# Seven block products for eight in the projections of a two-layer decoder trunk, with the first mixer in two stages and the last projection in one

## The chip, the cores and the metric

The kernel runs on one core of a Trainium2 chip. The metric is device time in microseconds (us) of one execution; three runs stand for the kernel before. The engines are TensorE (PE: matmuls, and transposes as matmuls), VectorE (DVE), ScalarE (ACT), GpSimd (POOL) and SyncE (SP, which issues the loads and stores). [...]

## The reference

1024 tokens of 1024 channels, with 16 learned meta tokens ahead of them (1040 in all), pass two layers, each with a norm ahead and a residual add behind. All is float32.

```python
hn = rmsnorm(h, norm_w[0])                     # layer 0: pooling mixer
v, gate = jnp.split(hn @ w_in, 2, axis=-1)     # w_in 1024 x 4096
u = trailing_mean(v, window 2/4/8/16 by group) - v
u = jnp.einsum('blgc,gcd->blgd', u, w_grp) * scale      # 4 groups of 512
h = h + (u * silu(gate)) @ w_out               # w_out 2048 x 1024
hn = rmsnorm(h, norm_w[1])                     # layer 1: HGRN2, 16 heads of 128
q, f, i, gate = jnp.split(hn @ w_in, 4, axis=-1)        # w_in 1024 x 8192
f = lb + (1 - lb) * sigmoid(f);  k = (1 - lb) * sigmoid(-f)
S_t = diag(f_t) S_{t-1} + k_t i_t^T;  o_t = S_t^T silu(q_t)
o = rmsnorm per head(o) * o_norm
h = h + (o * silu(gate)) @ w_out               # w_out 2048 x 1024
out = rmsnorm(h[16:], final_norm_w)
```

## The kernel before

Each float32 operand is split into hi + lo, both exact in the matmul's type: ACT casts hi (L209), DVE subtracts for lo (L210). A product is then three matmuls, whi with xhi, whi with xlo, wlo with xhi (`mm3`, L204 to L206). Tokens stand in the free dimension, channels in the partitions. x, transposed and split, lies in `xhi` and `xlo` for all of layer 0, the normed hn in the same place for layer 1; weights are prepared two ahead (`tick`, `need`).

Layer 0 (`mixer0`) goes by groups: four v tiles of 128 columns of w_in with their pooling (`v_tile`), then twice two gate tiles, their group projection (`grp_part`) and their part of the out projection, added into `acc` in SBUF (`out_part`, L360). Each tile takes the tokens in three chunks of 400, 384 and 256 columns (`CH0`), 24 matmuls each (8 channel blocks x 3), and a bank of PSUM for each chunk; four banks (`mm`) are for this, four (`at`) for transposes and the recurrence. `between` transposes h, makes the second norm, keeps h in DRAM and splits hn.

Layer 1 (`mixer1`) has 16 heads with four tiles each, f and i over all tokens in `CH0`, q and g in two chunks of 512. The recurrence of a head is cut into pieces (running product of the gates L601 and its reciprocal L602, scores L617, rectangles L573, turned K, states L700, outputs L719 and L720, gated output L734 to L737), which `later` places in the slots between the next head's projections. The gated output goes to `a_dram`. The last projection runs over heads 0 to 7 for all tokens and then over heads 8 to 15, with the weights of one half in SBUF (L781 to L783); behind each token tile of the second half come the final norm and the store.

The order on each engine is that of the program as the framework's scheduler leaves it; engines wait for one another by semaphores.

Of the kernel before, what the change touches and what calls it, by code (L numbers as in the profile page):

```python
# [8 lines left out]
F32 = mybir.dt.float32  # L9
# [5 lines left out]
P = 128  # L15
D = 1024
# [5 lines left out]
E = 2048  # L22
WINDOWS = (2, 4, 8, 16)
# [5 lines left out]
HALO = 16  # L29
# slots behind a head's last projection at which the pieces of its recurrence are issued  # L30
SCAN = (0, 1, 2, 3, 5, 7)
# [7 lines left out]
def kernel(  # L39
# [17 lines left out]
    vec, act, pool, pe = nc.vector, nc.scalar, nc.gpsimd, nc.tensor  # L57

    cst = ctx.enter_context(tc.tile_pool(name="cst", bufs=1))
    big = ctx.enter_context(tc.tile_pool(name="big", bufs=1))  # L60
    wp = ctx.enter_context(tc.tile_pool(name="wp", bufs=3))
    ps_mm = ctx.enter_context(tc.tile_pool(name="ps_mm", bufs=4, space=bass.MemoryType.PSUM))
    ps_at = ctx.enter_context(tc.tile_pool(name="ps_at", bufs=4, space=bass.MemoryType.PSUM))

# [3 lines left out]
    def mmbank():  # L68
        return ps_mm.tile([P, 512], F32, tag="mm", name="mm")
# [14 lines left out]
    def rstd_into(r, ssq, tn, n, dim):  # L84
        vec.tensor_scalar(r[:tn, :n], ssq[:tn, :n], 1.0 / dim, EPS, ALU.mult, ALU.add)  # L85
        pool.tensor_tensor(r[:tn, :n], r[:tn, :n], nhalf[:tn, :n], ALU.pow)  # L86
# [5 lines left out]
    stage = cst.tile([P, 4, HALO + L], F32, tag="stage", name="stage")  # L92
    raws = cst.tile([P, 2, 1024], F32, tag="raws", name="raws")
    nraw = [0]

    def ring(pool_, n, first=0):
        # n buffers in turn, the first four on the staging tile
        slots = [stage[:, i] for i in range(4)]
        slots += [pool_.tile([P, HALO + L], F32, tag=f"t{i}", name="t") for i in range(4, n)]
        at = [first]  # L100

        def get(name):
            at[0] += 1
            return slots[(at[0] - 1) % n]

        return get

    # per-channel vectors, turned so that the channel is the partition
    def load_tok(i, xt):
        t0, tn = TT[i]  # L110
        nc.sync.dma_start(xt[:tn], meta_tokens if i == 0 else x[t0 - META : t0 - META + tn])
        return xt

    w_in0 = pool_w_in[0].rearrange("(k p) n -> p k n", p=P)
    vr = [raws[:48, 1, :P], raws[:32, 1, P : 2 * P]]
    toks = {}
    nc.sync.dma_start(vr[0][0:32], hgrn_lb_logits.rearrange("a (k p) -> (a k) p", p=P))
    nc.sync.dma_start(vr[0][32:48], norm_w.rearrange("a (k p) -> (a k) p", p=P))
    toks[0] = load_tok(0, stage[:, 0, :D])
    toks[1] = load_tok(1, stage[:, 1, :D])  # L120
    nc.sync.dma_start(raws[:, 0].rearrange("p (a b) -> p a b", b=P), w_in0[:, :, :P])
    toks[2] = load_tok(2, stage[:, 2, :D])
    toks[3] = load_tok(3, stage[:, 3, :D])
# [74 lines left out]
    def prep_w(views, scale=None):  # L198
        return split_w(load_w(views), scale)
# [666 lines left out]
```

## Time and profile before

| | |
|---|---|
| runs | 1802.2, 1802.86 (median), 1804.11 us |
| span of the profiled execution | 1802.3 us |
| PE busy | 1778.4 us, 99% of the span |
| DVE, ACT, POOL busy | 1032.2 (57%), 551.5 (31%), 47.9 us (3%) |
| matmuls of the projections (L204 to L206) | 25% of the chain for each of the three lines |
| moved through HBM | 88.71 MB read, 16.78 MB written, 59 GB/s |
| granted clock of PE, mean | 0.998 |

Busy time of PE is modelled from pipelined matmuls, and a matmul's listed duration overlaps the next one's. What a matmul costs in a row of them is the distance between two starts. [...]

### The profile page before, as it was taken

What the parts mean: (1) busy time and instruction counts of PE and PEld (TensorE: products, weight loads), DVE (VectorE), ACT (ScalarE), POOL (GpSimd) and SP (SyncE); (2) the same over time, 40 slices, a digit from 0 to 9 for tenths busy, and PEclk for the clock granted to TensorE, in tenths of its full rate; (3) what the DMA queues carried; (4) which work ended last, traced back from release to release, by engine and by line L of the source; (5) the groups of instructions that cost most, each with busy time, mean ns of one, the idle gap of its engine ahead of it and who ended that gap; (6) DMA issues with size and microseconds to landing.
All of it is one profiled execution on the core that took longest, in us unless ns stands there. A gap on an engine that the chain in (4) does not pass through costs nothing.

```text
span 1802.3 us, 26333 instructions
## 1 busy us (share of the span) xinstructions
PE 1778.4 (99%) x11015; PEld 1649.4 (92%) x11015; DVE 1032.2 (57%) x1720; ACT 551.5 (31%) x1372; POOL 47.9 (3%) x68
## 2 busy tenths in 40 slices
PE   7999999999999999999999999999999999999998
PEld 7999999999999988899988999898989999888886
DVE  6765665685577568645564465546564555553433
ACT  6222322221222245232323333243323332232221
POOL 1000000000000000000000000000000000000000
PEclk9999999999999999999999999999999999999999
DMA  4111111111111113111111111121111111143421
GB/s 155 57 33 53 48 48 48 47 47 36 47 52 55 48 71 114 40 47 52 53 38 47 48 47 36 48 83 47 48 47 47 47 48 36 47 140 97 126 94 61
DMA packets 133823, 107.26 MB, mean 60 GB/s; under 512 B 3424, under 2 KB 122288, under 8 KB 133696
## 3 DMA queue, kind: packets, MB, share of 16 engines
q1 hardware_dynamic: 133696, 105.50, 19.0%
q8 instruction: 88, 1.44, 0.3%
q14 instruction: 39, 0.32, 0.1%
HBM read 88.71 MB, written 16.78 MB: 59 GB/s over the span
## 4 chain that ended last, share of the span: by engine, by line
PE 96%; ACT 1%; DVE 1%; POOL 0%; issue 0%; DMA 0%; SPq 0%; POOLq 0%; DVEq 0%; ACTq 0%
PE mm L204 25%; PE mm L206 25%; PE mm L205 25%; PE mm L781 3%; PE mm L783 3%; PE mm L782 3%; PE at L573 2%; PE at L700 2%; PE at L720 2%; PE at L617 2%; PE at L719 2%; PE at L539 1%; PE at L734 1%; PE at L684 1%; POOL rstd L86 0%
## 5 line engine op out<-in xcount | busy, mean ns | idle before, releaser
L204 PE MATMUL mm<-xhi,whi 128*128 128x400 f32 (+3 forms) x2048 | 704.0, 344 | 0.7 <-ACT xhi L209 0.7
L205 PE MATMUL mm<-xlo,whi 128*128 128x400 f32 (+3 forms) x2048 | 696.3, 340 | 0.2
L206 PE MATMUL mm<-xhi,wlo 128*128 128x400 f32 (+3 forms) x2048 | 695.9, 340 | 0.0
L204 PEld LDWEIGHTS mm<-xhi,whi 128*128 128x128 f32 x2048 | 385.3, 188 | 25.3 <-ACT xhi L209 1.3
L206 PEld LDWEIGHTS mm<-xhi,wlo 128*128 128x128 f32 x2048 | 386.2, 189 | 22.5
L205 PEld LDWEIGHTS mm<-xlo,whi 128*128 128x128 f32 x2048 | 385.7, 188 | 22.7 <-DVE xlo L210 0.9
L210 DVE TENSOR_TENSOR wlo<-raws,whi 128x1024 fp32r<-128x1024 f32 x88 | 107.5, 1222 | 116.8 <-ACT whi L209 116.7
L209 ACT CAST whi<-raws 128x1024 fp32r<-128x1024 f32 x88 | 92.4, 1050 | 257.6 <-PE mm L205 257.6
L360 DVE TENSOR_TENSOR acc<-acc,mm 128x400 f32<-128x400 f32 (+2 forms) x192 | 97.4, 514 | 57.9 <-PE mm L206 57.1
L204 PE MATMUL mm<-ah,whi 128*128 128x400 f32 (+2 forms) x384 | 124.8, 325 | 0.0
L205 PE MATMUL mm<-al,whi 128*128 128x400 f32 (+2 forms) x384 | 123.5, 322 | 0.0
L206 PE MATMUL mm<-ah,wlo 128*128 128x400 f32 (+2 forms) x384 | 123.1, 321 | 0.0
L192 ACT ACTIVATE whi<-raws,vecs 128x128 fp32r<-128x128 f32 x256 | 78.3, 390 | 143.2 <-PE mm L205 133.8
L86 POOL TENSOR_TENSOR rstd<-rstd,nhalf 128x1 f32<-128x1 f32 (+2 forms) x42 | 43.0, 1024 | 1705.0 <-DVE rstd L85 1702.4
L193 DVE SCALAR_TENSOR_TENSOR wlo<-raws,vecs,whi 128x128 fp32r<-128x128 f32 x256 | 75.2, 345 | 4.6 <-ACT xhi L166 2.8
L204 PEld LDWEIGHTS mm<-ah,whi 128*128 128x128 f32 x384 | 72.6, 189 | 0.2 <-DVE acc L360 0.2
L206 PEld LDWEIGHTS mm<-ah,wlo 128*128 128x128 f32 x384 | 72.7, 189 | 0.0
L205 PEld LDWEIGHTS mm<-al,whi 128*128 128x128 f32 x384 | 72.7, 189 | 0.0
L785 DVE TENSOR_TENSOR hres<-hres,mm 128x512 f32<-128x512 f32 x32 | 21.9, 686 | 85.6 <-PE mm L783 85.6
L736 DVE SCALAR_TENSOR_TENSOR G<-at,vecs,G 128x512 f32<-128x512 f32 x32 | 22.6, 746 | 82.9 <-PE at L734 82.9
L504 DVE TENSOR_SCALAR F<-F,oml,lb 128x400 f32<-128x400 f32 (+2 forms) x48 | 21.6, 454 | 73.0 <-ACT F L502 73.0
L206 PE MATMUL mm<-uh,wlo 128*128 128x400 f32 (+2 forms) x192 | 61.7, 321 | 0.0
(192 smaller groups left out, 2391.8 us busy)
## 6 DMA issues: line engine op xcount, KB each, us to landing
raws<-in_hgrn_w_in_dram SPq DMA_DIRECT2D x64, 512.0 KB, 3.9
raws<-in_pool_w_in_dram SPq DMA_DIRECT2D x32, 512.0 KB, 3.9
raws<-in_pool_w_out_dram SPq DMA_DIRECT2D x16, 512.0 KB, 3.6
a_dram<-G SPq DMA_DIRECT2D x16, 512.0 KB, 2.9
araw<-a_dram SPq DMA_DIRECT2D x16, 512.0 KB, 4.2
raws<-in_hgrn_w_out_dram SPq DMA_DIRECT2D x16, 512.0 KB, 3.9
raws<-in_pool_w_grp_dram SPq DMA_DIRECT2D x8, 512.0 KB, 3.3
hres<-h_dram SPq DMA_DIRECT2D x8, 512.0 KB, 4.2
```

The lines of the kernel that those rows point to most:

```text
L86: pool.tensor_tensor(r[:tn, :n], r[:tn, :n], nhalf[:tn, :n], ALU.pow)
L192: act.activation(hi[:, s], raw[:, s], AF.Copy, scale=scale[:, k : k + 1])
L193: vec.scalar_tensor_tensor(lo[:, s], raw[:, s], scale[:, k : k + 1], hi[:, s].bitcast(F32), ALU.mult, ALU.subtract)
L204: pe.matmul(ps, lhsT=wh, rhs=xh, start=i == 0, stop=False)
L205: pe.matmul(ps, lhsT=wh, rhs=xl, start=False, stop=False)
L206: pe.matmul(ps, lhsT=wl, rhs=xh, start=False, stop=i == n - 1)
L209: act.copy(hi, src)
L210: vec.tensor_tensor(lo, src, hi.bitcast(F32), ALU.subtract)
L360: vec.tensor_tensor(acc[:, m, s], acc[:, m, s], ps[:, :cn], ALU.add)
L781: pe.matmul(ps, lhsT=ah[:, n], rhs=wh[:, ws], start=n == 0, stop=False)
L782: pe.matmul(ps, lhsT=ah[:, n], rhs=wl[:, ws], start=False, stop=False)
L783: pe.matmul(ps, lhsT=al[:, n], rhs=wh[:, ws], start=False, stop=n == 7)
```

## The change

The input projections of both layers become block products. Two column tiles of weights (v and gate of one index, q and g, or f and i of one head) and the eight channel blocks make a matrix of 2 x 2 blocks (A); the channels in two halves and the tokens of one half of all (520) in two chunks of 260 columns (`CH`) make another (B). `pair` makes the seven weight operands, four of them with additions of 512 columns on DVE, `make_T` the seven token operands in hi + lo, which stay in SBUF for all tiles. `products` runs the seven in the order of `PRODUCTS`, both token halves with the same weights: 4 channel blocks x 3 matmuls x 2 chunks. Two double banks of PSUM take them: P1, P6, P7 and P4 add up in one, P2, P5 and P3 in the other, and after each product ACT copies or DVE adds what stands there.

```diff
-CH0 = ((0, 400), (400, 384), (784, 256))
-CHQ = ((16, 512), (528, 512))
+CH = 260
+PT = 2 * CH
...
+PRODUCTS = ("P1", "P2", "P6", "P5", "P7", "P3", "P4")
+OPENS = ("P1", "P2", "P5")
+BANK_A = ("P1", "P6", "P7", "P4")
...
+LOOK = 3
...
+        def pair(view1, view2):
+            i1, i2 = rawid(view1), rawid(view2)
+            st = {}
...
+            def p1():
+                ensure(i2)
+                return split_w(blocks()[0])
+            def p2():
+                return split_w(blocks()[1])
+            def p6():
+                a11, a12, a21, a22 = blocks()
+                s1, s2 = (half(n).rearrange("p a b -> p (a b)")[:, :512] for n in ("S1", "S2"))
+                st["s1"], st["s2"] = s1, s2
+                vec.tensor_tensor(s1, a21, a22, add)
+                vec.tensor_tensor(s2, s1, a11, sub)
+                return split_w(s2)
...
+            def p5():
+                ensure(i2 + 1)
+                return split_w(st["s1"])
+            def p7():
+                a11, a12, a21, a22 = blocks()
+                vec.tensor_tensor(a21, a11, a21, sub)
+                return split_w(a21)
...
+            def p3():
+                a11, a12, a21, a22 = blocks()
+                vec.tensor_tensor(a12, a12, st["s2"], sub)
+                return split_w(a12)
...
+        def make_T(p, src, R, w):
...
+            def norm(i):
+                t = unit("hn").rearrange("p (k t) -> p k t", k=2)
+                for j in range(2):
+                    k = 2 * i + j
+                    vec.scalar_tensor_tensor(t[:, j], src[i][:, j], w[:, k : k + 1], R, mul, mul)
+                hn[i] = t.rearrange("p k (c t) -> p k c t", c=2)
...
+            def put(name, srcs):
+                hi, lo = (unit(f"T{s}", F32R).rearrange("p (k t) -> p k t", k=4) for s in "hl")
+                for i, s in enumerate(srcs):
+                    n = s.shape[1]
+                    split(hi[:, i * n : (i + 1) * n], lo[:, i * n : (i + 1) * n], s)
+                T[name][p] = (hi, lo)
...
+            def s1():
+                norm(0), norm(1)
+                put("P1", B(0, 0))
+
+            def s2():
+                norm(2), norm(3)
+                put("P2", B(1, 0))
+
+            def s3():
+                diff("1", B(0, 1), B(0, 0))
+                diff("2", B(1, 1), halves(d["1"]))
+                put("P6", [d["2"]])
+
+            def s4():
+                put("P5", [d["1"]])
+                diff("4", B(1, 0), halves(d["2"]))
+
+            def s5():
+                diff("3", B(1, 1), B(0, 1))
+                put("P7", [d["3"]])
+
+            def s6():
+                put("P3", B(1, 1))
+                put("P4", [d["4"]])
+
+            return [s1, s2, s3, s4, s5, s6]
+        def products(passes, m, m2):
+            s = slice(passes[0], passes[-1] + 1)
+            a = x_ = None
+            for name in PRODUCTS:
+                w = need()
+                if name == "P1":
+                    a = mmbanks()
+                elif name == "P2":
+                    x_ = mmbanks()
+                b = a if name in BANK_A else x_
+                for p in passes:
+                    th, tl = T[name][p]
+                    for k in range(4):
+                        ks = slice(k * P, (k + 1) * P)
+                        o = b[:, p, :CH]
+                        first = name in OPENS and k == 0
+
+                        kw = dict(skip_group_check=True)
+                        pe.matmul(o, lhsT=w[:, 0, ks], rhs=th[:, k], start=first, stop=False, **kw)
+                        pe.matmul(o, lhsT=w[:, 0, ks], rhs=tl[:, k], start=False, stop=False, **kw)
+                        pe.matmul(o, lhsT=w[:, 1, ks], rhs=th[:, k], start=False, stop=k == 3, **kw)
+                bs = b[:, s, :CH]
+                if name in ("P1", "P6", "P5"):
+                    t = half(name)
+                    act.copy(t[:, s], bs)
+                    if name == "P1":
+                        p1 = t
+                    elif name == "P6":
+                        u2 = t
+                    else:
+                        p5 = t
+                elif name == "P2":
+                    m(s, 0, bs, p1[:, s])
+                elif name == "P7":
+                    m2(s, 1, bs, p5[:, s])
+                elif name == "P3":
+                    m(s, 1, bs, u2[:, s])
+                else:
+                    m2(s, 0, bs, None)
+                tick()
```

Norm weights go into the token operands, not into the weights. Layer 0 first makes v and gate of all 16 pairs, and keeps the pooled u and the gate in DRAM (`u_dram`, `s_dram`). Then, for one token half after the other, `grp_stage` makes the group projection and `out_stage` the out projection, both with chunks of 260; their weights are loaded for each half. x comes back from `x_dram`. The second norm of the first half is spread over the second half's stages, that of the second half over head 0.

```diff
+        def grp_stage(p):
+                for k in range(4):
+                    ur = half("ur").rearrange("p a b -> p (a b)")
+                    nc.sync.dma_start(ur, u_dram[g * 4 + k][:, p * PT : (p + 1) * PT])
+                    u = unit("u", F32R).rearrange("p (h t) -> p h t", h=2)
+                    split(u[:, 0], u[:, 1], ur)
+                    us.append(u)
+                for j in range(4):
+                    w = need()
+                    sg = half("sgh")
+                    m = g * 4 + j
+                    nc.sync.dma_start(sg.rearrange("p a b -> p (a b)"), s_dram[m][:, p * PT : (p + 1) * PT])
+                    ps = mmbanks()
+                    mm3(ps, w, us, True, True)
+                    vec.scalar_tensor_tensor(sg, ps[:, :, :CH], pscale[:, m : m + 1], sg, mul, mul)
+                    at = unit("a", F32R).rearrange("p (h t) -> p h t", h=2)
+                    split(at[:, 0], at[:, 1], sg.rearrange("p a b -> p (a b)"))
+                    a[m] = at
+                    tick()
...
+        def out_stage(p, a):
+            for m in range(KD):
+                    h = unit("h").rearrange("p (k t) -> p k t", k=2)
+                    nc.sync.dma_start(h, x_dram[m : m + 2, :, p * PT : (p + 1) * PT].rearrange("k p t -> p k t"))
+                ps = mmbanks()
+                for q in range(4):
+                    mm3(ps, need(), [a[4 * q + i] for i in range(4)], q == 0, q == 3)
+                    tick()
+                o = hs[-1][:, m % 2].rearrange("p (c t) -> p c t", c=2)
+                vec.tensor_tensor(o, o, ps[:, :, :CH], add)
...
+        steps = prologue(1)
+        spread(steps)
+        c0 = v_gate(0)
+        products((0,), *c0)
+        flush()
+        products((1,), *c0)
+        for t in range(1, ME):
+            products((0, 1), *v_gate(t))
+        flush()
+        a = grp_stage(0)
+        hs = out_stage(0, a)
+        spread(between(0, hs))
+        a = grp_stage(1)
+        hs = out_stage(1, a)
+        flush()
+        mixer1(between(1, hs))
```

In layer 1 the gate g of a head goes to `g_dram`, and the output `og` without it to `a_dram`. The last projection takes all 16 heads in one accumulation, in four blocks of 256 tokens, and loads and multiplies a and g for each head and block; the weights are loaded and split in the first block. The reciprocals are four of 260 columns (L693).

```diff
-                    vec.scalar_tensor_tensor(G[:, s], b, onorm[:, n : n + 1], G[:, s], mul, mul)
-                nc.sync.dma_start(a_dram[n], G)
+                        act.activation(og[:, b0 * P : b0 * P + 512], b, AF.Copy, scale=onorm[:, n : n + 1])
+                    nc.sync.dma_start(a_dram[n], og)
...
+                    for i in range(4):
+                        s = slice(i * CH, (i + 1) * CH)
+                        vec.reciprocal(iX[:, s], X[:, s])
...
+            def prep(r, n):
+                if r == 0:
+                    raw = rawtile()
+                    nc.sync.dma_start(raw, hgrn_w_out[0, n * P : (n + 1) * P])
+                    wh, wl = unit("woh", F32R), unit("wol", F32R)
+                    split(wh[:, :D], wl[:, :D], raw)
+                    wo[n] = (wh, wl)
+                ar, gr = (half(t).rearrange("p a b -> p (a b)")[:, :256] for t in ("ar", "gr"))
+                ts = slice(r * 256, r * 256 + 256)
+                nc.sync.dma_start(ar, a_dram[n][:, ts])
+                nc.sync.dma_start(gr, g_dram[n][:, META + r * 256 : META + r * 256 + 256])
+                vec.tensor_tensor(ar, ar, gr, mul)
+                w = wslot()
+                split(w[:, 0, :256], w[:, 1, :256], ar)
+                return w
...
+            for r in range(NR):
+                ps = None
+                for n in range(HEADS):
+                    fetch(r * HEADS + n + 3)
+                    if ps is None:
+                        if r % 2 == 0:
+                            ps = [[t[:, 0], t[:, 1]] for t in (mmbanks(), mmbanks())]
...
+                    for i in range(2):
+                        ts = slice(i * P, (i + 1) * P)
+                        for nh in range(2):
+                            s = slice(nh * 512, nh * 512 + 512)
+                            pe.matmul(ps[i][nh], lhsT=w[:, 0, ts], rhs=wh[:, s], start=n == 0, stop=False)
+                            pe.matmul(ps[i][nh], lhsT=w[:, 0, ts], rhs=wl[:, s], start=False, stop=False)
+                            pe.matmul(ps[i][nh], lhsT=w[:, 1, ts], rhs=wh[:, s], start=False, stop=n == HEADS - 1)
```

How rows move on the engines, at three places:

PE, the first instructions behind the branch. L164 and L400 are transposes of x, L214 and L151 the broadcast of a token's norm, L204 to L206 the first tile. Before:

```order
L164 MATMUL at<-ident,stage 128x16 x8
L164 MATMUL at<-ident,stage 128x128 x8
L134 MATMUL at<-ident,raws 128x32
L164 MATMUL at<-ident,stage 128x128 x16
L204 MATMUL mm<-xhi,whi 128x400
L205 MATMUL mm<-xlo,whi 128x400
L214 MATMUL at<-ident,rstd 128x16
L206 MATMUL mm<-xhi,wlo 128x400
L204 MATMUL mm<-xhi,whi 128x400
L205 MATMUL mm<-xlo,whi 128x400
L206 MATMUL mm<-xhi,wlo 128x400
L204 MATMUL mm<-xhi,whi 128x400
```

Now (L338 to L340 are the first product, of the first token half):

```order
L400 MATMUL at<-ident,xt 128x16 x8
L151 MATMUL at<-ident,rstd 128x16
L400 MATMUL at<-ident,xt 128x128 x8
L151 MATMUL at<-ident,rstd 128x128
L400 MATMUL at<-ident,xt 128x128 x8
L151 MATMUL at<-ident,rstd 128x128
L400 MATMUL at<-ident,xt 128x128 x8
L151 MATMUL at<-ident,rstd 128x128
L400 MATMUL at<-ident,xt 128x120 x8
L151 MATMUL at<-ident,rstd 128x120
L338 MATMUL mm<-Th,w 128x260
L339 MATMUL mm<-Tl,w 128x260
```

Before, the first tile's matmuls stand between the broadcasts; now all transposes and broadcasts of a half stand ahead of its first product, whose right operand (`Th`, `Tl`) is made from the normed tokens.

DVE, the hand-over from one group to the next in the group projection. L344 and L486 scale the product and multiply with the gate, L210 and L147 are the subtractions for lo. Before, at the first chunks of a group:

```order
L344 SCALAR_TENSOR_TENSOR stage<-mm,vecs,stage 128x400
L210 TENSOR_TENSOR al<-stage,ah 128x400
L287 MEMSET stage 128x16
L344 SCALAR_TENSOR_TENSOR stage<-mm,vecs,stage 128x400
L210 TENSOR_TENSOR al<-stage,ah 128x400
L344 SCALAR_TENSOR_TENSOR stage<-mm,vecs,stage 128x384
L210 TENSOR_TENSOR al<-stage,ah 128x384
L344 SCALAR_TENSOR_TENSOR stage<-mm,vecs,stage 128x384
```

Now, at the end of one group (`a`, `w`: gated product and weights; `u`: the operands of the next group):

```order
L486 SCALAR_TENSOR_TENSOR sgh<-mm,vecs,sgh 128x520
L147 TENSOR_TENSOR w<-raw,w 128x512
L147 TENSOR_TENSOR a<-sgh,a 128x520
L486 SCALAR_TENSOR_TENSOR sgh<-mm,vecs,sgh 128x520
L147 TENSOR_TENSOR w<-raw,w 128x512
L147 TENSOR_TENSOR a<-sgh,a 128x520
L147 TENSOR_TENSOR u<-ur,u 128x520 x4
L486 SCALAR_TENSOR_TENSOR sgh<-mm,vecs,sgh 128x520
L147 TENSOR_TENSOR w<-raw,w 128x512
L147 TENSOR_TENSOR a<-sgh,a 128x520
```

The four u subtractions of the next group stand behind the last gated product of this one; before, u of a group was split a tile at a time behind its pooling.

DVE, a head's scan and reciprocals (L601 and L602 before, L690 and L693 now), with F's last gate ahead and q behind. Before:

```order
L504 TENSOR_SCALAR F<-F,oml,lb 128x256
L599 COPY Zt<-F 128x65
L600 MEMSET F 128x65
L601 SCALAR_TENSOR_TENSOR stage<-F,Zt 128x1040
L602 RECIPROCAL stage<-stage 128x1040
L517 SCALAR_TENSOR_TENSOR Q<-mm,oml,stage 128x512
L704 COPY stage<-at 128x128
L606 TENSOR_TENSOR K<-K,stage 128x1040
```

Now (`P_` numbers are copied products, `mm` the bank; L633 and L636 make F, L611 and L613 q of the next head):

```order
L147 TENSOR_TENSOR w<-S_8878,w 128x512
L633 TENSOR_TENSOR F<-P_8696,mm 128x2x260
L147 TENSOR_TENSOR w<-raw,w 128x512
L636 TENSOR_SCALAR F<-F,oml,lb 128x2x260
L688 COPY Zt<-F 128x65
L689 MEMSET F 128x65
L690 SCALAR_TENSOR_TENSOR X<-F,Zt 128x1040
L147 TENSOR_TENSOR w<-raw,w 128x512
L693 RECIPROCAL F<-X 128x260 x4
L611 TENSOR_TENSOR Q<-P_8913,mm 128x2x260
L696 TENSOR_TENSOR Q<-Q,X 128x1024
L613 SCALAR_TENSOR_TENSOR Q<-Q,oml,sig 128x2x260
```

Behind the reciprocals now stands the add of the next head's first q product from its bank, and a weight subtraction stands between scan and reciprocals.

## Rows read from the trace of the kernel before

**Rows 1.** The page's list of busy engines, and its group of POOL's powers:

```profile
PE 1778.4 (99%) x11015; PEld 1649.4 (92%) x11015; DVE 1032.2 (57%) x1720; ACT 551.5 (31%) x1372; POOL 47.9 (3%) x68
...
L86 POOL TENSOR_TENSOR rstd<-rstd,nhalf 128x1 f32<-128x1 f32 (+2 forms) x42 | 43.0, 1024 | 1705.0 <-DVE rstd L85 1702.4
```

**Rows 2.** Windows: busy us (and count) of each engine, clock, DMA:

```profile
0.00:36.00 36.00, 26.59 (x140) 22.74 (x141) 20.17 (x59) 26.18 (x62) 8.07 (x31) 1.00 0.48 164
640.00:700.00 60.00, 54.35 (x337) 49.33 (x336) 42.39 (x96) 34.10 (x82) 5.56 (x9) 0.97 0.28 97
726.90:785.10 58.20, 58.20 (x379) 52.62 (x379) 31.60 (x42) 18.33 (x50) 1.65 (x1) 1.00 0.16 46
```

**Rows 3.** Timeline of PE in layer 0: start, duration, line, shape:

```profile
100.46 0.34 PE L204 MATMUL mm<-uh,whi 128*128 128x384 f32 x1
...
104.67 0.34 PE L204 MATMUL mm<-ah,whi 128*128 128x400 f32 x1
...
113.31 0.28 PE L204 MATMUL mm<-uh,whi 128*128 128x256 f32 x1
...
115.67 0.28 PE L206 MATMUL mm<-uh,wlo 128*128 128x256 f32 x1
```

**Rows 4.** Timeline of PE, one column tile of head 1:

```profile
729.72 0.39 PE L205 MATMUL mm<-xlo,whi 128*128 128x512 f32 x1
...
735.05 0.34 PE L204 MATMUL mm<-xhi,whi 128*128 128x400 f32 x1
```

**Rows 5.** The chain of waits, start and length of its pieces:

```profile
677.24 1.71 PE at L395 x8
...
726.88 1.78 PE at L617 x16
...
785.09 1.78 PE at L617 x16
```

**Rows 6.** Timeline of PE in the last projection, to its last matmul:

```profile
1785.21 0.39 PE L781 MATMUL mm<-wo_h,ah 128*128 128x512 f32 x1
...
1786.34 0.39 PE L783 MATMUL mm<-wo_h,al 128*128 128x512 f32 x1
...
1793.14 0.39 PE L783 MATMUL mm<-wo_h,al 128*128 128x512 f32 x1
```

**Rows 7.** Timeline of DVE in one head:

```profile
741.93 0.69 DVE L564 TENSOR_TENSOR Q<-Q,Fe 128x512 f32<-128x512 f32 x1 [1.29 <-PE at L573]
742.54 0.68 DVE L565 TENSOR_TENSOR K<-K,Fe 128x512 f32<-128x512 f32 x1
...
752.64 2.33 DVE L601 TENSOR_TENSOR_SCAN stage<-F,Zt 128x1040 f32<-128x1040 f32 x1
755.00 6.65 DVE L602 RECIPROCAL stage<-stage 128x1040 f32<-128x1040 f32 x1
```

**Rows 8.** DVE by line and shape: busy us, mean ns, idle before:

```profile
L210 DVE TENSOR_TENSOR wlo<-raws,whi 128x1024 fp32r<-128x1024 f32 x88 | 107.5, 1222 | 116.8 <-ACT whi L209 116.7
```

**Rows 9.** DMA issues: queue, count, size, us to landing:

```profile
raws<-in_hgrn_w_in_dram SPq DMA_DIRECT2D x64, 512.0 KB, 3.9
...
a_dram<-G SPq DMA_DIRECT2D x16, 512.0 KB, 2.9
...
t<-in_x_dram SPq DMA_DIRECT2D x2, 512.0 KB, 5.5
```

**Rows 10.** ACT by line and shape, the gates' sigmoid:

```profile
L516 ACT ACTIVATE stage<-mm 128x512 f32<-128x512 f32 x18 | 10.7, 597 | 31.8 <-PE mm L206 31.8
```

**Rows 11.** Windows, the stretch that moves most bytes:

```profile
6.00:10.00 4.00, 2.84 (x16) 2.40 (x16) 1.81 (x5) 2.29 (x8) 0.00 (x0) 1.00 1.07 410
```

**Rows 12.** Timeline of PE at the start:

```profile
17.14 0.54 PE L204 MATMUL mm<-xhi,whi 128*128 128x400 f32 x1
...
18.80 0.54 PE L206 MATMUL mm<-xhi,wlo 128*128 128x400 f32 x1
```

More of the change, by code (lines that the diff above doesn't have):

```diff
@@ L22 @@
 E = 2048
+ME = E // P
 WINDOWS = (2, 4, 8, 16)
@@ L382, in between, with load_tokens @@
-        def between(c0, cn):
-            tiles = [(t0, tn) for t0, tn in TT if c0 <= t0 < c0 + cn]
-            rb = None
-            for t0, tn in tiles:
-                ssq, r = small("ssq"), small("rstd", 6)
-                if not hts:
-                    hts.extend(t0tile("ht") for _ in range(4))
-                hts.append(hts.pop(0))
-                ht = hts[0]
+        def load_tokens(p):
+            out_ = []
+            for t0, tn in TP[p]:
+                xt = unit("xt")
+                if t0 == 0:
+                    nc.sync.dma_start(xt[:tn, :D], meta_tokens)
+                else:
+                    nc.sync.dma_start(xt[:tn, :D], x[t0 - META : t0 - META + tn])
+                out_.append(xt)
+            return out_
@@ new lines, in mm3 @@
+        def mm3(ps, w, xs, first, last):
+            for k in range(4):
+                ks = slice(k * P, (k + 1) * P)
+                for c in range(2):
+                    cs = slice(c * CH, (c + 1) * CH)
+                    o = ps[:, c, :CH]
+                    pe.matmul(o, lhsT=w[:, 0, ks], rhs=xs[k][:, 0, cs], start=first and k == 0, stop=False)
+                    pe.matmul(o, lhsT=w[:, 0, ks], rhs=xs[k][:, 1, cs], start=False, stop=False)
+                    pe.matmul(o, lhsT=w[:, 1, ks], rhs=xs[k][:, 0, cs], start=False, stop=last and k == 3)
@@ new lines, in spread, with flush, early @@
+        def spread(steps, gap=1, first=0):
+            for i, fn in enumerate(steps):
+                later(first + i * gap, fn)
+        def flush():
+            while due:
+                now[0] += 1
+                for fn in due.pop(now[0] - 1, []):
+                    fn()
+        def early(n, tiles, view):
+            for t in list(range(n)) * 2 + list(range(n, tiles)):
+                pair(*view(t))
+        early(1, ME, lambda t: (cols(w_in0, t), cols(w_in0, ME + t)))
+        for _ in range(2):
+            feed_grp()
+            feed_out()
@@ new lines, in whole @@
+        early(1, 2 * HEADS, lambda t: head_views(t // 2)[t % 2])
+        for fn in prologue(0):
+            fn()
+        fill()
+        if fast:
+            later(40, make_mask)
+        steps = prologue(1)
+        spread(steps)
+        c0 = v_gate(0)
[4 more added lines that the diff above has]
+            products((0, 1), *v_gate(t))
+        flush()
+        a = grp_stage(0)
+        hs = out_stage(0, a)
+        spread(between(0, hs))
```

1096 lines of the change are left out of this document (495 added, 601 removed).

## The prediction

> **What bounds the kernel now.** I read the page's busy list first: TensorE (PE) has 1778.4 of 1802.3 us, VectorE (DVE) 57% [rows 1]. The table by windows says where the missing 24 us lie: PE is full in a stretch such as one head (58.20 of 58.20), and is not in the first 36 us (26.6) and from 640 to 700 us (54.4) [rows 2]; the rest lies behind the last matmul. So the kernel lasts as long as its matmuls, and a matmul as long as its step, start to start. That I read from the timeline: 24 steps of 384 columns take 4.21 us (0.175), 48 of 400 take 8.64 (0.180), 20 of 256 take 2.36 (0.118) [rows 3]; in a head 23 steps of 512 take 5.33 (0.232) [rows 4]. Weight loads are inside these steps. The chain of waits meets the same line of successive heads 58.2 us apart [rows 5].
>
> Before, in these terms: layer 0 has 32 tiles x 24 x (0.180 + 0.175 + 0.118) = 363.6 us, its group projection 192 x 0.473 = 90.9, its out projection 384 x 0.473 = 181.8; together 636.3. A head is 24 x (2 x 0.473 + 4 x 0.232) = 45.0 of projections; the remaining 13.2 of 58.2 are pieces of the recurrence. The last projection is 768 steps of 0.226 = 173.6 (5 take 1.13), and from the end of the last matmul, 1793.5, to the end 8.8 pass [rows 6]. Going back from the end (8.8, 173.6, 1 between, 16 x 58.2) head 0 begins near 687.5. So layer 0 has 687.5 - 636.3 = 51 us that are not its projections: start, transposes, second norm.
>
> **The change, part by part.**
>
> *Products.* A pair of column tiles needs 7 products of 24 matmuls of 260 columns. The trace has no 260; between 256 and 400 a column costs 0.43 ns, so 0.118 + 0.0017 = 0.1197 us. Bounds: 0.118, no dearer than 256, and 0.122, since the step of 384 lies 2.3 ns over that line. A pair takes 168 x 0.1197 = 20.1 us. Layer 0: 16 pairs, 321.8 for 363.6, **-41.8**. Heads: 32 pairs, 643.5 for 16 x 45.0 = 719.5, **-76.0**. Group and out projection in the same chunks: 2304 x 0.1197 = 275.8 for 272.7, **+3.1**. The bounds shift all of this by -18 to +24. The last projection keeps 768 matmuls of 512 columns. The arithmetic alone gives -115.
>
> *The start.* Work moves to DVE. Per half of the tokens the operands take 8 norms, 8 differences and 6 subtractions of 520 columns and 4 subtractions of 1040. Back to back 512 columns take 0.61 [rows 7]; 1024 have a duration of 1.22 [rows 8], so a step near 1.15: 22 x 0.62 + 4 x 1.15 = 18 us. The tokens are loaded only behind the branch (near 6 us), land 5.5 us later [rows 9], and pass transposes, a square sum, POOL's power and a broadcast: the first norm starts near 22 us. From there DVE has 2 x 18 us of operands, 2.5 weight sets of 11 instructions at 0.61 (17 us), and copies, small ones and adds (8): 61 us. The first product of tile 1 needs the second half's operands, so it starts near 83. Of that time 20 us are tile 0's products: 63 of overhead. Bounds 45, if the second half's operands are done in step with the products, and 75. Tiles of window 16, the ones with most adds, cost some 2 more.
>
> *Two stages.* In the group stage a group's four u are split behind the last group's gated product. PE's next matmul waits for scale, w, a and u in DVE's order (the second place shown), 4 x 0.6 and a cast: 2.75 us, three times; and about 5 us at the first, for the store and the reload through DRAM (2.9 and 3.9 us [rows 9]): 13.5. In the second half's stage the norm of the first is spread: DVE has 16 x 4 instructions at 0.61 (39 us) and 18 of operands, and since the norms come through PE, ACT and POOL one after another some 11 more: 68 us for PE's 46, 22 of overhead. The two out stages: 1. Head 0 must have the second half's operands: five token tiles, each with transposes of 1.71 [rows 5], about 1.2 of ACT, 1.02 of POOL [rows 1] and a broadcast, 4.5 together, then 23 us of operands and splits; of these 45 us PE has work for 25: 20 us. Layer 0's overhead: 63 + 2 + 13.5 + 22 + 1 + 20 = 121.5 for 51, **+70.5** (bounds +30, where all but the start is hidden, and +95).
>
> *Heads.* DVE has 31.6 us of work in 58.2 [rows 2]. Four weight subtractions of 1.22 [rows 8] leave; 22 instructions of 512 columns at 0.69 come (+10.3), the adds of two products per output about +4, the gate's product leaves for the end (-1.5): 44.4 us in a head of 40.2 + 13.2 = 53.4, or 83%. One place is dear: scan and reciprocals, 2.33 + 6.65 us in one piece [rows 7], with the add of the next q behind them (the third place shown). From the end of P3 DVE's way to that add is add, two sigmoids of about 0.6 [rows 10], scale, small ones, scan, a weight, reciprocals, add: 13.0 us. PE meanwhile has P4, P1, P2 and P6 (11.5) and the transposes of V (1.0), and then wants the bank: 0.5 us late. With 0.4 at the rectangles 0.9 a head, **+14.4** (bounds 0 and 48, 3 us a head).
>
> *Last projection.* In its first token block each head's weights are split as they come, 16 steps of 2.7 us with 768 KB loaded in each. That is 290 GB/s against 410 moved from 6 to 10 us [rows 11], so I count no bandwidth. Its fourth weight stands behind head 15's reciprocals (4.4 us), head 15's own output goes through norm, store and reload (3.8), others 0.9: **+9** (bounds 4 and 15). At the end the first tile's norm stands in DVE ahead of the second's adds, 12 us for 8.8: **+3**.
>
> *Sum:* 1802.3 - 41.8 - 76.0 + 3.1 + 70.5 + 14.4 + 9 + 3 = 1784.5, on the profiled execution. The runs' median lies 0.6 above its span, so 1785: a gain of 1%. Of the 115 some 97 are paid back, 70 of them in layer 0.
>
> **The rivals.** A measurement of this kernel can tell 0.2% (3.6 us) from no change.
>
> 1. *The arithmetic arrives.* If the hand-overs between stages lie beside PE's work, layer 0's overhead is at its lower bound and the rest is gone: 1802 - 115 + 30 = 1717. For it: the waits in the stages hang on DVE's order, and DVE's sums there fill the time only just. Against: in the second norm's stretch of before, with less for DVE to do, PE already lost 5.6 of 60 us [rows 2]. 0.13.
>
> 2. *Two double banks hold PE in the heads: slower.* Four single banks took the tiles in turn before. Now a product starts only when the reader of the bank two products earlier is done, and DVE, which is most of these readers, is 83% full. The place is the q add behind the reciprocals, and the adds of the next products behind it. By my count DVE has no room left there, so a microsecond by which a sigmoid or a weight comes later is paid 16 times. It decides from 18/16 = 1.1 us a head beyond my 0.9. With 2.5 us, one scan more ahead of the add: 1785 + 40 = 1825. Against: DVE has 9 us a head left elsewhere, in which it catches up. 0.20.
>
> 3. *The clock falls.* [...] Against: the 5.6 us of gaps before cost 3% of clock in 60 us. 0.06. [...]
>
> 4. *Small matmuls save nothing*, if a weight load holds each. At the step of 384 columns (0.175) the 10368 matmuls of 260 would cost 573 us more, some 2350 in all; 11 ns more each already take the 115 back. Against: the 256-column steps of 0.118 [rows 3], each with its own load. 0.01.
>
> **How the numbers follow.** Forecast, 1760 to 1799: 0.55; rival 1: 0.13; rivals 2 to 4: 0.27; the sum ending within 3.6 us of before: 0.05. The likeliest gives 1785. Faster is 0.55 + 0.13 and 0.02 of the mild ends of rivals 2 and 3, 0.70; same 0.05 and 0.01 of these ends, 0.06; slower 0.24. The range leaves out a tenth on either side, below most of rival 1, above what of rivals 2 to 4 goes beyond the prices given: 1740 to 1825.
>
> **What would show it.** Right: steps of 260 columns near 0.120; the first product of tile 1 near 83 us; in the group stages PE waiting for DVE's u and a, stages of about 59 and 68 us; 20 us of gaps ahead of and in the first products of head 0; heads 54 us apart; 9 us of waits in the last projection's first block; 12 us behind the last matmul. Wrong: heads of 56 us or more with matmuls waiting for adds (rival 2), a granted clock under 0.9 in a stage (rival 3), group stages of 46 us (rival 1).

## The result and the profile after

The changed kernel takes 1863.97 us (median of 4 runs, 1860.17 to 1864.24) against 1803.05: a ratio of 1.033, 95% interval 1.0315 to 1.0345. It is 3.3% slower, where 1% faster was forecast. The page of the profiled execution, answering to [rows 1]:

```profile
span 1862.5 us, 32892 instructions
...
PE 1718.2 (92%) x13531; PEld 1648.1 (88%) x13531; DVE 1256.9 (67%) x2018; ACT 756.9 (41%) x1696; POOL 49.4 (3%) x70
```

PE has 60 us less work than before, and the span is 60 us longer: 144 us of it PE is not busy, for 24 before. The windows by stage (columns as in [rows 2]; the granted clock is a share of full speed): most of tile 0's first and second half, steady tiles, first and second group stage, head 0, a later head, first block of the last projection and its other three.

```profile
36.00:70.00 34.00, 22.90 (x120) 20.71 (x121) 24.66 (x47) 16.40 (x32) 2.19 (x4) 1.00 0.29 95
70.00:101.00 31.00, 20.68 (x98) 18.18 (x96) 27.87 (x47) 14.98 (x27) 5.39 (x5) 0.67 0.27 95
120.00:400.00 280.00, 280.00 (x2331) 280.00 (x2330) 200.46 (x298) 99.33 (x205) 0.00 (x0) 1.00 0.33 108
404.00:470.00 66.00, 54.91 (x391) 53.08 (x390) 47.26 (x70) 28.98 (x51) 0.00 (x0) 0.87 0.69 225
562.00:647.50 85.50, 61.48 (x436) 59.02 (x435) 59.81 (x100) 43.31 (x83) 3.17 (x5) 0.82 0.51 164
739.00:812.00 73.00, 55.72 (x392) 51.82 (x391) 51.53 (x95) 38.99 (x82) 3.16 (x5) 0.84 0.25 80
867.00:922.50 55.50, 53.74 (x476) 52.64 (x475) 43.03 (x67) 26.07 (x65) 1.65 (x1) 1.00 0.19 58
1644.50:1717.40 72.90, 63.17 (x330) 50.61 (x331) 50.95 (x78) 32.25 (x70) 1.64 (x1) 0.93 0.52 172
1717.40:1850.50 133.10, 133.10 (x577) 107.96 (x575) 51.86 (x126) 25.95 (x68) 3.45 (x6) 1.00 0.44 137
```

The steady tiles are full, at a clock of 1.00. Most of the loss lies in the start and the hand-overs, where PE is busy for 67 to 83% and the clock is down to 0.67, some in each head and in the last projection's first block. The timeline of PE gives the marks: tile 1, the last matmul of layer 0's products, out stage, second group stage, its out stage, head 0, head 1, the heads' last product, last projection, its last matmul.

```profile
101.40 0.28 PE L338 MATMUL mm<-Th,w 128*128 128x260 f32 x1
...
404.35 0.28 PE L340 MATMUL mm<-Th,w 128*128 128x260 f32 x1
...
469.97 0.29 PE L499 MATMUL mm<-a,w 128*128 128x260 f32 x1
...
561.97 0.28 PE L499 MATMUL mm<-u,w 128*128 128x260 f32 x1
...
647.54 0.28 PE L499 MATMUL mm<-a,w 128*128 128x260 f32 x1
...
739.31 0.28 PE L338 MATMUL mm<-Th,w 128*128 128x260 f32 x1
...
811.91 0.28 PE L338 MATMUL mm<-Th,w 128*128 128x260 f32 x1
...
1643.27 0.28 PE L340 MATMUL mm<-Th,w 128*128 128x260 f32 x1
1644.50 0.50 PE L920 MATMUL mm<-woh,w 128*128 128x512 f32 x1 [0.95 <-ACT woh L146]
...
1850.20 0.40 PE L922 MATMUL at<-woh,w 128*128 128x512 f32 x1
```

The fifteen tiles from 101.40 to one step behind 404.35 take 20.2 us each, or 0.1203 for each of 168 steps. The first group stage lasts 65.6 us (404.35 to 469.97), the second 85.6, head 0 72.6; the fifteen heads from 811.91 to one step behind 1643.27 take 55.4 on average (most of them 55.5). What PE waited for, in the list of waits (us in total, times, longest):

```profile
PE at L151 <- POOL rstd L104: 34.1, 18, 4.2
PE mm L499 <- ACT u L146: 25.2, 6, 11.0
PE mm L338 <- DVE Q L611: 23.3, 15, 1.7
PE mm L338 <- ACT Th L146: 18.9, 11, 3.0
...
PE mm L921 <- DVE wol L147: 4.6, 2, 3.9
PE mm L920 <- ACT w L146: 4.3, 1, 4.3
```

### The profile page after: what moved, and what is told of

The parts are those of the page before. It is cut to its first block, busy times and chain, and to the rows that moved or that the text cites. A ratio compares the mean times of both kernels' runs of the same rounds, so it can differ in the third digit from the quotient of the medians.

```text
span 1862.5 us, 32892 instructions
## 1 busy us (share of the span) xinstructions
PE 1718.2 (92%) x13531; PEld 1648.1 (88%) x13531; DVE 1256.9 (67%) x2018; ACT 756.9 (41%) x1696; POOL 49.4 (3%) x70
## 4 chain that ended last, share of the span: by engine, by line
PE 75%; DVE 12%; ACT 6%; issue 4%; POOL 2%; DMA 1%; SPq 0%; DVEq 0%; ACTq 0%; POOLq 0%
PE mm L338 14%; PE mm L340 13%; PE mm L339 13%; PE mm L500 5%; PE mm L499 5%; PE mm L501 5%; DVE F L693 4%; PE at L662 2%; POOL rstd L104 2%; PE at L920 2%; PE at L922 2%; PE at L921 2%; PE at L708 2%; PE at L807 2%; ACT on L834 2%
## 5 line engine op out<-in xcount | busy, mean ns | idle before, releaser
L338 PE MATMUL mm<-Th,w 128*128 128x260 f32 x2688 | 782.3, 291 | 43.2 <-DVE Q L611 23.3
L339 PE MATMUL mm<-Tl,w 128*128 128x260 f32 x2688 | 768.1, 286 | 5.4 <-DVE Tl L147 5.3
L340 PE MATMUL mm<-Th,w 128*128 128x260 f32 x2688 | 768.3, 286 | 0.0
L338 PEld LDWEIGHTS mm<-Th,w 128*128 128x128 f32 x2688 | 513.5, 191 | 52.4 <-DVE Q L611 26.4
L339 PEld LDWEIGHTS mm<-Tl,w 128*128 128x128 f32 x2688 | 513.7, 191 | 8.0 <-DVE Tl L147 7.9
L340 PEld LDWEIGHTS mm<-Th,w 128*128 128x128 f32 x2688 | 513.7, 191 | 0.7
L146 ACT CAST w<-raw 128x512 fp32r<-128x512 f32 x346 | 207.0, 622 | 256.0 <-PE mm L501 193.5
L147 DVE TENSOR_TENSOR w<-raw,w 128x512 fp32r<-128x512 f32 x346 | 232.0, 685 | 117.0 <-ACT w L146 116.4
L344 ACT COPY P<-mm 128x520 f32<-128x520 f32 (+1 forms) x150 | 85.8, 572 | 185.9 <-PE mm L340 185.6
L499 PE MATMUL mm<-a,w 128*128 128x260 f32 x512 | 145.2, 284 | 0.0
L500 PE MATMUL mm<-a,w 128*128 128x260 f32 x512 | 144.3, 282 | 0.0
L501 PE MATMUL mm<-a,w 128*128 128x260 f32 x512 | 143.8, 281 | 0.0
L693 DVE RECIPROCAL F<-X 128x260 f32<-128x260 f32 x64 | 106.9, 1733 | 0.0
L147 DVE TENSOR_TENSOR w<-S,w 128x512 fp32r<-128x512 f32 x100 | 67.5, 686 | 57.1 <-ACT w L146 57.1
L499 PE MATMUL mm<-u,w 128*128 128x260 f32 x256 | 78.4, 311 | 25.2 <-ACT u L146 25.2
L501 PEld LDWEIGHTS mm<-a,w 128*128 128x128 f32 x512 | 96.3, 188 | 0.0
L500 PEld LDWEIGHTS mm<-a,w 128*128 128x128 f32 x512 | 96.3, 188 | 0.0
L499 PEld LDWEIGHTS mm<-a,w 128*128 128x128 f32 x512 | 96.1, 188 | 0.0
L500 PE MATMUL mm<-u,w 128*128 128x260 f32 x256 | 78.3, 307 | 2.9 <-DVE u L147 2.8
L499 PEld LDWEIGHTS mm<-u,w 128*128 128x128 f32 x256 | 53.7, 212 | 26.7 <-ACT u L146 26.4
```

The source lines that it names most:

```text
L146: act.copy(hi, src)
L147: vec.tensor_tensor(lo, src, hi.bitcast(F32), sub)
L338: pe.matmul(o, lhsT=w[:, 0, ks], rhs=th[:, k], start=first, stop=False, **kw)
L339: pe.matmul(o, lhsT=w[:, 0, ks], rhs=tl[:, k], start=False, stop=False, **kw)
L340: pe.matmul(o, lhsT=w[:, 1, ks], rhs=th[:, k], start=False, stop=k == 3, **kw)
L344: act.copy(t[:, s], bs)
```

## The experiments

One theory and its rivals stood at first. Theory A: the orders on the engines hold PE, each at a place that can be named. The rivals: VectorE's total load (whatever the order), the double banks (of PSUM, the `mm` that PE's matmuls write), and the clock. Each experiment is one profiled execution unless a median is given; base is the changed kernel, 1862.5 us of span.

**Reciprocals a slot later.** Code: the four reciprocals in a piece of their own behind the next head's P2.

```diff
...
-PIECES = {"run": 0, "turn_v": 1, "scale": 2, "score": 4, "l32": 5, "l64": 6, "turn_k": 7, "states": 8, "outs": 10, "gated": 12}
+PIECES = {"run": 0, "turn_v": 1, "recip": 1, "scale": 2, "score": 6, "l32": 7, "l64": 8, "turn_k": 9, "states": 10, "outs": 12, "gated": 14}
...
```

> The changed kernel with the four reciprocals of a head one slot later, behind the next head's first q add, and the pieces from the scores on two slots later; no work is left out. Theory A (the q add behind scan and reciprocals holds P5, 1.65 us a head in the trace): the wait of the products for the q add goes, a head takes 53.6 to 54.3 us for 55.5, the kernel some 18 to 28 us less than 1862.5. Rival B (the wait only moves: with VectorE at 83% some other add is late next): heads stay at 55.0 to 56, less than 8 us gained.

Span 1858.5, most heads 54.9 to 55.3: what rival B said. But the edit did only half of what it says. DVE's timeline of this run shows that the scheduler still put two reciprocals ahead of the q add (L611):

```profile
1036.36 3.41 DVE L695 RECIPROCAL F<-X 128x260 f32<-128x260 f32 x2
1039.69 0.64 DVE L611 TENSOR_TENSOR Q<-P,mm 128x520 f32<-128x520 f32 x1
1040.25 1.76 DVE L695 RECIPROCAL F<-X 128x260 f32<-128x260 f32 x1
```

The wait for that add fell from 1.65 to 0.5 us; 0.8 us of gaps appeared at the gated output's transposes, the product behind them and the rectangles, all pieces that had been moved. So it does not decide between the theories.

**No reciprocals.** The loop of L691 to L693 is left out; K is scaled by the gates in place of their products' reciprocals.

> Leaves out the four reciprocals of each head (K is scaled by the gates themselves in their place), 6.7 us of VectorE work a head, order otherwise as in the changed kernel. Theory A: heads at 53.5 to 53.9 us, the products' and score pieces' bare time, and 6 us less in the last projection's first block; 28 to 38 us off the 1862.5. Rival B (two double banks hold PE at every reader, wherever VectorE stands): heads lose less than half of their 2 us over that bare time, 55.5 to not below 54.6.

Span 1827.5, heads 53.5 to 53.6 us apart, and no wait for L611 is left in the list. Theory A: nothing else in a head holds PE, double banks and 7 readers a pair included.

**First half's norm over the out stage.**

```diff
-        spread(between(0, hs))
+        steps = between(0, hs)
         a = grp_stage(1)
+        spread(steps)
         hs = out_stage(1, a)
```

> The norm and operands of the first token half are spread over the second half's out stage in place of its group stage; nothing left out. Theory A (VectorE's 57 us of work and the chain of norms hold the group stage): second group stage 62 to 67 us for 85.5, as the first (65.6 with the start), second out stage 92 to 97 for 91.7, head 0 unchanged: 15 to 24 us less. Rival B (the stage is slow by itself, from the reload through DRAM and the clock): second group stage stays above 78, or the out stage pays it back; under 8 us.

Span 1843.3, 19.2 us less. The second group stage takes 56.1 us for 85.6, its out stage 101.6 for 91.8. Two windows of this run, one over the group stage (559.6 to 615.7 us), 1.3 us late, and one over 92 us of the out stage:

```profile
561.00:617.00 56.00, 49.83 (x393) 48.38 (x392) 39.95 (x60) 25.96 (x44) 0.00 (x0) 0.97 0.59 190
617.00:709.00 92.00, 88.60 (x732) 87.52 (x731) 50.12 (x84) 35.61 (x70) 2.75 (x5) 1.00 0.40 121
```

DVE's work moved to a stage that had room (50 of these 92 us, for 33 of 92 in the changed kernel), at a price of 10 us there. Theory A, and stronger than expected, since the group stage falls below the first half's.

**Dummy matmuls in the gaps.**

```diff
...
+                if len(passes) == 1:
+                    fillers(5)
                 for p in passes:
...
+        def fillers(n):
+            b = atbank()
+            for _ in range(n):
+                pe.matmul(b[:, :P], lhsT=ident, rhs=ident, start=True, stop=True)
...
```

> Adds dummy matmuls of 128 x 128 with the identity on PE, ahead of each wait of the start, of the group stages' first products, of the token norms and of the half products (5 to 8 each, 1.1 to 1.8 us at full clock); they compute nothing that is used. Theory C (the granted clock of 0.5 to 0.8 makes these stretches longer than summed): the clock stays at 0.9 or more there, first product of tile 1 at 88 to 94 us for 101.4, second group stage 72 to 78 for 85.5, head 0 62 to 67 for 72.6, together 20 to 35 us less. Rival D (VectorE's and ACT's chains set these stretches, the clock only follows from the gaps): the stretches stay within 3 us or grow by the fillers' time, the kernel 0 to 25 us slower.

Span 1875.9, 13 us more. Two stretches of this run, from the first product of the second token half to the next pair's first: in tile 0 and in head 0.

```profile
80.80:104.45 23.65, 22.67 (x192) 22.20 (x190) 23.65 (x36) 11.63 (x20) 6.64 (x4) 1.00 0.12 37
...
779.93:804.90 24.97, 20.93 (x148) 20.01 (x146) 24.29 (x39) 12.30 (x21) 0.00 (x0) 0.86 0.13 37
```

Without fillers the same two took 24.9 us at a clock of 0.61 and 23.3 us at 0.64. The clock is 1.00 and 0.86 now, and the stretches are about as long. VectorE is busy for nearly all of both (23.65 of 23.65 us, 24.3 of 25.0; without fillers 22.7 and 21.3): here the low clock went with the gaps and did not make them, as rival D said. The fillers cost PE time of their own, so a gain smaller than theirs is not excluded. The other stages do not decide it: the first group stage took 63.2 us for 65.6, the second 89.6 for 85.6, all of head 0 80.6 for 72.6. In the window from 36 to 70 us the clock was 0.75 where it had been 1.00; why was not tried.

**Eight products, all else kept.** Weights without combinations, four token operands, outputs in banks of their own:

```diff
...
+            for put in (m, m2):
+                banks = (mmbanks(), mmbanks())
+                for kk in range(2):
+                    w = need()
+                    for c in range(2):
+                        for p in passes:
+                            th, tl = T[f"{kk}{c}"][p]
...
```

> The changed kernel with the seven products undone and all else kept: eight products of the plain blocks, each output in a bank of its own, four weight splits a pair and no combinations, four token operands in place of seven; same stages, same chunks of 260, nothing left out. PE then has 48 pairs x 24 x 0.120 = 138 us more. Theory A (the seven products do save, and what the stages and VectorE take back is mostly the two-stage structure, not the combinations): 60 to 90 us of the 138 remain, 1920 to 1950. Rival B (the combinations cost as much as they save: VectorE's part in the start, in the stages and in the heads goes with them): under 20 us more, 1850 to 1880.

Span 1940.7 (1942.55 timed). Of the 138 us that the eighth product is worth 78 show, as Theory A said; heads are 59.85 apart for 55.5. The group stages are little better without the combinations, 62.5 us for 65.6 and 78.5 for 85.6: most of their cost is that of the two-stage structure. The start is another matter: with four token operands in place of seven, tile 1 begins at 89.0 us for 101.4, though tile 0 has more matmuls.

**u a group ahead.** The four loads and splits of the next group's u beside the second and third product of a group.

```diff
...
+                    if g < 3 and 0 < j < 3:
+                        nxt += [load_u(g + 1, 2 * j - 2), load_u(g + 1, 2 * j - 1)]
```

> The u of the next group are loaded and split beside the second and third product of a group, not behind the fourth; nothing left out. Theory A (hand-overs of the group stages wait for loads and splits in VectorE's and ACT's order, 25 us in 6 waits, the longest 11): the first group stage 65.6 to 55 to 60 us, the second 85.5 to 76 to 82; 8 to 15 us less in all. Rival B (VectorE's total in the stages decides, not the order): under 4 us.

Span 1838.9: group stages 52.8 and 71.6 us for 65.6 and 85.6. The wait of PE for ACT's u fell from 25.2 us in six to 3.6 in one; four waits for the gated product, 10.0 us, are new. Theory A, with twice the gain expected. Half of the first stage's gain is not a wait, as its window shows beside that of the changed kernel (404 to 470 us):

```profile
404.00:456.40 52.40, 47.85 (x384) 47.65 (x385) 45.64 (x69) 28.48 (x50) 0.00 (x0) 0.97 0.86 278
```

PE idles 4.6 us for 11.1, and it is busy for 47.9 us for 54.9 with the same matmuls of the stage, at a clock of 0.97 for 0.87.

**Broadcast behind the next transposes.**

```diff
...
-            rb = atbank()
-            rbcast(rb[:, :tn], r, tn)
-            vec.tensor_copy(R[:, t0 : t0 + tn], rb[:, :tn])
+            def bcast():
+                rb = atbank()
+                rbcast(rb[:, :tn], r, tn)
+                vec.tensor_copy(R[:, t0 : t0 + tn], rb[:, :tn])
+            behind.append(bcast)
...
```

> The broadcast of a token tile's norm is issued behind the next tile's transposes, in the start and in the second norm, so that PE does not stand at POOL's power; nothing left out. Theory A (in PE's order each token tile's transposes stand behind the broadcast of the tile before, 5.2 us a tile in a chain through ACT, VectorE and POOL; 34 us of PE waits): first product at 26 to 30 us for 36.0, tile 1 at 88 to 94 for 101.4, second group stage and head 0 each 3 to 8 us less; 15 to 28 us in all. Rival B (VectorE's operands set these stretches): tile 1 above 97, under 7 us in all.

Span 1838.3: first product at 26.4 us for 36.0, tile 1 at 90.8 for 101.4, second group stage 78.1, head 0 69.0. Theory A. The chain of waits of the changed kernel shows what was undone: transposes of successive token tiles 5.0 to 5.2 us apart, with ACT and POOL between them.

```profile
12.92 1.91 PE at L400 x8
...
17.94 1.72 PE at L400 x8
...
21.37 0.94 POOL rstd L104
23.15 1.72 PE at L400 x8
```

**The three orders together.** 

> The three orders together: the first half's norm spread over the out stage, u a group ahead, broadcasts behind the next transposes. If they work apart from one another, 19 from the norm and the sum of what the other two give: 1810 to 1830 for 1862.5, still above the kernel before. Rival (they wait for the same engine and overlap): above 1835.

1803.96 us (median of 10), ratio to before 1.0002 (0.9992 to 1.0011): a tie, 6 us under the range that was expected. By spans (1802.8) the three give 59.7 of the 67.0 us that they gave singly. The second group stage is at 46.0 us, its matmuls' bare time.

**Scan and reciprocals in two parts.** Blocks of 16 tokens whose gates are ready behind P2 at once, the others where all stood:

```diff
...
+                    if fast and c == 0:
+                        later(0, lambda: run((0, 256), (528, 768)))
...
-                return {"run": run, "scale": scale, "score": score}
+                return {"run": lambda: run((256, 528), (768, L)), "scale": scale, "score": score}
...
```

> The changed kernel with scan and reciprocals of a head in two parts: blocks of 16 tokens whose gates are ready behind P2 (496 columns) are done beside P6 to P3, the other 544 where all stood before; nothing left out, the same columns. Theory A (one piece of 9 us ahead of the q add): VectorE's way to the add is 4.3 us shorter, the wait of 1.65 us a head goes, heads at 53.5 to 53.9 us for 55.5, 24 to 32 us less than 1862.5 with the last head's share. Rival B (VectorE's total of 83%, a wait that only moves as in the run with the later reciprocals): heads above 54.6.

Span 1826.0, heads 53.5 to 53.6, as without reciprocals, with all the work done; 36.5 us less, where 24 to 32 were expected. VectorE is busy for 44.8 of the 55.5 us from 867 to 922.5, more than the 43.0 of the changed kernel, and PE is full there. Theory A; the rival of VectorE's total load falls. The same place in DVE's timeline:

```profile
865.48 1.34 DVE L638 TENSOR_TENSOR_SCAN X<-F,Zt 128x272 f32<-128x272 f32 x2
866.74 3.54 DVE L639 RECIPROCAL F<-X 128x272 f32<-128x272 f32 x2
870.19 1.16 DVE L698 TENSOR_TENSOR Q<-Q,X 128x1024 f32<-128x1024 f32 x1
...
872.42 0.69 DVE L611 TENSOR_TENSOR Q<-P,mm 128x520 f32<-128x520 f32 x1
```

4.7 us stand where 9.4 stood (from the scan to what follows the reciprocals), and PE waits for no q add in this run's list of waits.

**All four.** 

> The three orders of stages together (1803.96) and scan and reciprocals in two parts. If the heads' share adds up: 1772 to 1782, faster than the kernel before by 1.1 to 1.7%. Rival (head waits return at another place): 1790 to 1804.

1772.01 us (median of 5, 1770.51 to 1772.95), ratio to before 0.9826 (0.9812 to 0.9839): 1.7% faster than the kernel before, 92 us faster than the changed one.

```profile
span 1771.2 us, 33031 instructions
...
PE 1697.7 (96%) x13531; PEld 1633.8 (92%) x13531; DVE 1251.9 (71%) x2162; ACT 752.6 (42%) x1696; POOL 49.5 (3%) x70
```

PE still idles 73 us. In the list of waits 18.5 of them are for the token operands' hi parts, in the start and head 0, 13.6 for norms.

**Lo parts of weights on GpSimd.** As the last, with `pool.tensor_tensor` for `vec.tensor_tensor` in `split_w`.

> As the run with all four orders, with the subtraction for the lo part of the projections' and of the out projections' weights (512 columns, 0.6 us on VectorE, 14 a head) on GpSimd, which is at 3%. Theory A (VectorE's load is what is left): start and head 0 shorter, 5 to 15 us less than that run. Rival B (GpSimd takes so long for 512 columns that weights come late, or slows VectorE): 10 to 150 us more.

Span 1836.8, 66 us more than without; heads 56.1. That is rival B. GpSimd takes 1.4 us for what took DVE 0.69, and instructions left on DVE are longer. In this run, a weight's lo on POOL and a token operand's on DVE:

```profile
L213 POOL TENSOR_TENSOR w<-raw,w 128x512 fp32r<-128x512 f32 x346 | 477.6, 1396 | 314.5 <-ACT w L212 296.6 <-issue 15.5 <-PE mm L339 2.4
...
L147 DVE TENSOR_TENSOR Tl<-T,Th 128x1040 fp32r<-128x1040 f32 x16 | 28.1, 1769 | 5.9 <-ACT Th L146 5.9
```

and that operand in the run before, with POOL idle:

```profile
L147 DVE TENSOR_TENSOR Tl<-T,Th 128x1040 fp32r<-128x1040 f32 x16 | 19.7, 1239 | 3.2 <-ACT Th L146 3.2
```

## Why the prediction was wrong

Products and heads went by the mechanism foretold, the heads at too small a price. The step that failed is layer 0's overhead, whose sum left out waits and the slower matmuls between them. Nearly all differences have one sign. Mark by mark, forecast and measured:

| part | forecast | measured | difference |
|---|---|---|---|
| first product of tile 1 | 83 | 101.4 | +18.4 |
| first group stage | 59.5 | 65.6 | +6.1 |
| second group stage | 68 | 85.6 | +17.6 |
| head 0 beyond its 40.3 of products | 20 | 32.3 | +12.3 |
| heads 1 to 15, apart | 54.3 | 55.4 | +17 in all |
| last projection, with the last pieces | 195.8 | 207.2 | +11 |
| behind the last matmul | 12 | 11.9 | 0 |

These are 82 us; tiles, out stages and rounding take back 4, and 1784.5 became 1862.5.

- *Products.* Right: 0.1203 a step for 0.1197, a pair 20.2 for 20.1, the out stages 92.0 and 91.8. The saved matmul time arrived but for some 5 us.
- *Layer 0's overhead* is the step that failed: 121.5 was forecast, about 174 measured, so not +70.5 but about +123. By stages:
- *The start.* I counted DVE's work and let the token tiles follow one another freely. They don't: in PE's order a tile's transposes stand behind the broadcast of the tile before, which waits for POOL. The broadcast run takes 10.6 us off the start; the other 8 were not separated.
- *First group stage.* The waits were about as counted, 11.1 us of idle PE for 13.5. What the sum left out is PE's own pace: it was busy for 54.9 us of the window, where 384 steps of 0.1203 make 46.2, at a clock of 0.87. The run with u ahead gives back some of both (47.9 us at 0.97); no run moved the clock alone there.
- *Second group stage.* 22 us for the spread norm were counted as PE's cost; 39 were measured, and the run that moves the norm shows 29.5 of them to go with it, 10 of which the out stage pays. PE idles 24.0 us, 11.0 of them in one wait for the third group's u. It is no wait for a load: ahead of it VectorE is at the norm's operands (hn, T) in the chain of waits, and in ACT's order the u casts, at 612.56 us, stand behind the cast of T.

```profile
598.76 2.07 DVE hn L270 x4
604.61 1.40 DVE hn L270 x3
609.74 1.83 DVE T L286 x3
```

```profile
613.24 0.80 PE L499 MATMUL mm<-u,w 128*128 128x260 f32 x2 [10.98 <-ACT u L146]
```

- *Head 0.* Of its 12.3 us the broadcast run takes 3.6; the rest was not separated.
- *Heads.* The place, the mechanism, the sign and VectorE's load (43.0 us a head for 44.4) were right, the size was not: 1.65 us at the q add where I counted 0.5. In DVE's timeline of one head (start, duration) and PE's product behind it:

```profile
863.71 0.69 DVE L147 TENSOR_TENSOR w<-S,w 128x512 fp32r<-128x512 f32 x1 [2.87 <-ACT w L146]
864.32 0.69 DVE L633 TENSOR_TENSOR F<-P,mm 128x520 f32<-128x520 f32 x1
...
866.82 0.55 DVE L636 TENSOR_SCALAR F<-F,oml,lb 128x520 f32<-128x520 f32 x1 [1.21 <-ACT F L635]
...
867.91 2.32 DVE L690 TENSOR_TENSOR_SCAN X<-F,Zt 128x1040 f32<-128x1040 f32 x1
...
870.73 6.68 DVE L693 RECIPROCAL F<-X 128x260 f32<-128x260 f32 x4
877.33 0.64 DVE L611 TENSOR_TENSOR Q<-P,mm 128x520 f32<-128x520 f32 x1
```

```profile
878.02 0.39 PE L338 MATMUL mm<-Th,w 128*128 128x260 f32 x1 [1.65 <-DVE Q L611]
```

PE's side was as counted: P3 ended near 863.7, the bank was wanted at 876.4, 12.6 us for 12.5. DVE's way to the end of the q add was 14.2 us and not 13.0: a weight subtraction stands ahead of F's add too, and the sigmoids took 1.8 us from add to scale, not 1.2. Rival 2 had the right place at two thirds of its price (1.65 us for 2.5); the bank order itself costs nothing that shows: without reciprocals heads are 53.5 to 53.6 us apart.
- *The clock* fell as rival 3 said, to 0.50 in the lowest 10 us (80 to 90 and 770 to 780 us). It was 0.67, 0.87, 0.82 and 0.84 in the windows of tile 0's second half, the two group stages and head 0, under the 0.9 that the prediction had named as this rival's sign. In the second half of tile 0 the fillers show it to be no cause (23.65 us at a clock of 1.00 for 24.9 at 0.61); in the first group stage the slower matmuls are 8 us of the loss. What it cost in all is open: in PE's timeline the 260-column steps of 0.17 to 0.35 us in the start, the group stages and head 0 add up to some 25 us more than at 0.1203, part of it beside VectorE's work. At the start of the kernel before, 5 steps of 400 columns took 1.66 us [rows 12], 0.332 each for 0.180 in [rows 3], and the clock listed for these 36 us is 1.00 [rows 2]; why was not tried. The four orders together gained 92 us at a mean clock of 0.973 for 0.970. The heads, with one pause for the q add in each (23.3 us in 15, the longest 1.7), stayed at 1.00, as from 867 to 922.5 us.
- *Last projection.* Some 16 us of stalls and slower steps in its first block for 9, and the 512-column steps took 0.231 (133.1 us for 576) where 0.226 was read before: 4 us.
- *Rival 1*, 1717 us, was not reached by the repaired orders either: they stand at 1772.

## What to carry to other kernels

Saved matmul time arrived here only where PE, which waits in its order, found its operands (a steady tile 20.2 us for 20.1 forecast, the second group stage 85.6 for 46.0 of bare matmuls). So price a hand-over by the whole chain (norm, broadcast, split) and by what stands ahead of it in each engine's order, not by the sum of one engine's work, and price the matmuls between gaps by the steps that a trace shows there (here 54.9 us of PE, at a clock of 0.87, where 46.2 were counted). A run of long instructions on one engine (here 9 us) is best cut where half of its input is ready earlier; that gave 36.5 us alone and 32 on top of the other three orders. And before an algebraic saving is judged, repair the orders around it: the same seven products were 3.3% slower than the kernel before, and 1.7% faster with four orders changed.

## What the runs showed of the hardware that was not expected

VectorE was slower beside GpSimd's elementwise work: with 446 subtractions on POOL, DVE's 128x1040 subtraction took 1769 ns for 1239. The 512-column matmul step was 0.231 us in the changed last projection and 0.226 in the one before, with the same shapes; the cause was not tried. With dummy matmuls ahead of PE's waits the granted clock was 1.00 for 0.67 from 70 to 101 us, and 0.75 for 1.00 from 36 to 70 us.
